# Row maxima and low-part scores of a two-mixer attention step, contracted over 64 rows and two heads at a time

## The chip, the cores and the metric

The kernel runs on one core of one Trainium2 chip. The metric is the device time of one execution in microseconds (us); before the change the median of three runs is 723.58 us. A core has five engines that run side by side, each in the order of its own instruction queue: PE (TensorE, the matrix multiplier: a matmul is a weight load followed by a stream of moving columns), DVE (VectorE), ACT (ScalarE), POOL (GpSimd) and SP, which here only issues DMAs. PE writes its results to PSUM, which has eight banks of 128 partitions by 512 float32; DVE and ACT read them there.

## The reference

One layer of a diffusion step: 128 context tokens and 1024 latent tokens are normalised, modulated, projected into queries, keys, values and gates of two mixers, attended, gated and projected out. Mixer A has 8 query heads on 2 key heads and looks at all keys; mixer B has as many, looks at a band of 128 to each side and adds a learned sink to each head's softmax. Both look at 128 cached context keys too. A head has 64 dimensions. Cut to what matters here:

```
def one_block(qblk):                       # mixer A, 128 queries, k_all = context and 1024 latent keys
    s = jnp.einsum('bqkgd,bskd->bkgqs', qblk, k_all).astype(jnp.float32) * (d ** -0.5)
    p = jax.nn.softmax(s, axis=-1).astype(v_all.dtype)
    return jnp.einsum('bkgqs,bskd->bqkgd', p, v_all)

# mixer B, banded blocks of 128 queries and up to 3 * 128 keys, and the context
s = jnp.concatenate([sink_column(sink, kv, s_ctx.shape[:-1]), s_ctx, s_band], axis=-1)
p = jax.nn.softmax(s, axis=-1).astype(v_lat.dtype)
o = p_ctx @ v_ctx + p_band @ v_band        # as einsums in the reference
```

Everything is float32.

## The kernel before

**Numbers.** PE multiplies a rounded float32 type. A float32 value is therefore kept as a high part, rounded to that type, and a low part, the rest. A query tile `qt` has 128 partitions and 4 heads of 128 queries: rows 0 to 63 hold the high part of the 64 dimensions, rows 64 to 127 the low part. The high keys `kha` (mixer A) and `khb` (mixer B) and the low keys of mixer B `klb` are stored twice, in rows 0 to 63 and again in rows 64 to 127. So one matmul over all 128 rows gives (high + low query) times high key; a second one over the low key completes a score.

**Units, slots.** The attention is cut into units: a block of 128 queries, a mixer, a key head (4 query heads). Units of mixer A (even numbers) and of mixer B (odd) alternate; 32 of latent queries, and 4 of the context. A unit of mixer A has nine slots, one for each block of 128 keys; one of mixer B has three or four. The main loop goes slot by slot and writes, for each, in this order on every engine: callbacks that fell due (`tick`), the slot's scores (`scores`), the items that a table put there (`due`), two or three matmuls of the output projection (`out_items`, line 1189), and the values (`values`, lines 1118 to 1121) of the slot three places back. The order is written out by hand in this way and each engine keeps it; nothing is rescheduled later.

**Scores of mixer A** are computed with keys on the partitions (lines 1097, 1098), exponentiated by ACT (1100), cut in two parts by ACT (1104) and POOL (1108), and multiplied with the values. A softmax needs a shift that is at or near the maximum of a row. It is made one unit ahead by `max_items`: for each of 4 heads and each of 3 groups of 384 keys a matmul with queries on the partitions (`pmx`, line 858) and a DVE reduction (859); twelve such items a unit. Their negated maxima are turned round by PE (`ptm`, 877) and spread by DVE into four rows of the tile `qb` (878), which is the moving operand of line 1098.

**Scores of mixer B** are made in `weight_items` with queries on the partitions, one head an item: a matmul with `khb` (915) and one with `klb` (916) into the same bank, a DVE operation that adds the mask and finds the negated row maximum (919), and one slot later ACT's exponential (905). The weights are turned round by PE (1092) in the unit's own slots, and the sums by `pti` (967).

**Banks.** Tag "A" of PSUM has two banks, handed out in turn. The maxima, the scores of mixer B, `ptm` and `pti` all use them: PE can start on the next one only when DVE or ACT has read the one before the last.

**Places.** `MX_AT` gives the slot of each maximum item, counted from the start of the mixer A unit before it; `NAT_AT` the slots of mixer B's items, counted from the start of the mixer A unit ahead. The items of units 0 and 2 run between the matmuls of the gate projection, before the slots. Query tiles are loaded by one DMA of SP each (838), at least five slots ahead of their first use.

Of the kernel before, what the change touches and what calls it, by code (L numbers as in the profile page):

```python
# [18 lines left out]
P = 128  # L19
# [20 lines left out]
LOADED = 4  # L40


NAT_AT = (0, 1, 2, 3)
NAT_FIRST = (0, 1, 2, 3)
MX_AT = (-4, -3, -2, -2, -1, 4, 5, 5, 7, 7, 8, 8)
MX_FIRST = (0, 1, 2, 2, 3, 4, 4, 5, 6, 6, 7, 8)
PH_DVE = 0
MX_END = 10
SPLIT_LAG = 2
# [58 lines left out]
def hybrid_step(ctx, tc, x_prompt, x_sample, cache_k_a, cache_v_a, cache_k_b, cache_v_b,  # L108
# [33 lines left out]
    def bank(tag, name):  # L142
        return ps.tile([P, 512], F32, tag=tag, name=name, bufs=BANKS[tag])
# [690 lines left out]
    def u_load(i):  # L834
        t, m, g = units[i]
        more = i % QTS > 3
        qt_ = (qp2[0] if more else qp).tile([P, 512], F32R, tag="qt", name=f"qt{i}", bufs=QTS - 4 if more else 4)
        nc.sync.dma_start(qt_.bitcast(F32), q_dram[t][m][:, 512 * g : 512 * g + 512])
        qtile[i] = qt_

    def max_items(i):

        t, m, g = units[i]
        out = []

        def item(h, b):
            if h == 0 and b == 0:
                mxtile[i] = qs.tile([P, 4, 3], F32, tag="mx", name=f"mx{i}", bufs=3)
            mx = mxtile[i]
            lhs = qtile[i][:, P * h : P * h + P]  # L850
            pm = bank("A", f"pmx{i}_{h}_{b}")
            if t == 0:
                for h in range(4):
                    hs = slice(P * h, P * h + P)
                    nc.tensor.matmul(pm[:, hs], qtile[i][:, hs], khp[:, g, :], start=True, stop=True)
                nc.vector.tensor_reduce(mx[:, :, 0], pm.rearrange("p (h n) -> p h n", h=4), axis=AX.X, op=ALU.max)
            else:
                nc.tensor.matmul(pm[:, 0:384], lhs, kha[:, g, 3 * b : 3 * b + 3, :], start=True, stop=True)  # L858
                nc.vector.tensor_reduce(mx[:, h, b : b + 1], pm[:, 0:384], axis=AX.X, op=ALU.max)  # L859

        def finish():
            qb_ = qp.tile([68, 512], F32R, tag="qb", name=f"qb{i}", bufs=2)
            nc.sync.dma_start(qb_[0:64, :].bitcast(F32), q_dram[t][m][0:64, 512 * g : 512 * g + 512])
            qbtile[i] = qb_
            mx = mxtile.pop(i)
            mn = m_nat[i // 2 % 2]
            if t > 0:
                m4 = qs.tile([P, 4], F32, tag="m4", name=f"m4{i}", bufs=3)
                nc.vector.tensor_reduce(m4, mx, axis=AX.X, op=ALU.max)
            else:  # L870
                m4 = mx[:, :, 0]
            nc.vector.tensor_scalar(mn, m4, -1.0, None, op0=ALU.mult)
            later(TURN, transpose)

        def transpose():
            pt = bank("A", f"ptm{i}")
            nc.tensor.transpose(pt[0:4, 0:P].bitcast(F32R), m_nat[i // 2 % 2], ident_r)
            nc.vector.tensor_tensor(qbtile[i][64:68, :].rearrange("p (h n) -> p h n", h=4),  # L878
                                    pt[0:4, 0:P].unsqueeze(1).to_broadcast([4, 4, P]),
                                    diag.unsqueeze(2).to_broadcast([4, 4, P]), op=ALU.mult)  # L880

        for h in range(4 if t else 1):
            for b in range(3 if t > 0 else 1):
                out.append(lambda h=h, b=b: item(h, b))
        return out, finish

    def weight_items(i):

        t, m, g = units[i]
        v = {}  # L890

        def small(name):
            return qs.tile([P, 4], F32, tag=name, name=f"{name}{i}")

        def first(n):
            if t:
                penat[i] = qp2[0].tile([P, 4, 512], F32, tag="pen", name=f"pen{i}")[:, :, 0:n]
            else:
                penat[i] = w3.tile([P, 512], F32, tag="pe", name=f"pen{i}", bufs=PES).rearrange(
                    "p (h n) -> p h n", h=4)  # L900
            for x in ("nm", "sum", "ex", "inv"):
                v[x] = small(x)

        def exp(h, s, scale):
            nc.scalar.activation(penat[i][:, h], s, AF.Exp, bias=v["nm"][:, h : h + 1], scale=scale,  # L905
                                 accum_out=v["sum"][:, h : h + 1])

        def item(h):
            p0, p1_ = window(t)
            n = P * (p1_ - p0)  # L910
            if h == 0:
                first(n)
            lhs = qtile[i][:, P * h : P * h + P]
            s = bank("A", f"sn{i}_{h}")[:, 0:n]
            nc.tensor.matmul(s, lhs, khb[:, g, p0:p1_, :], start=True, stop=False)
            nc.tensor.matmul(s, lhs, klb[:, g, p0:p1_, :], start=False, stop=True)  # L916
            m0 = P if t == 1 else 0

            nc.vector.tensor_tensor_reduce(s, s, mask[:, m0 : m0 + n], -1.0, nsink[:, 4 * g + h : 4 * g + h + 1],  # L919
                                           op0=ALU.add, op1=ALU.min, accum_out=v["nm"][:, h : h + 1])  # L920
            later(1, lambda: exp(h, s, -1.0))

        def prompt():
            first(P)
            s = bank("A", f"sn{i}")
            for h in range(4):
                hs = slice(P * h, P * h + P)
                nc.tensor.matmul(s[:, hs], qtile[i][:, hs], khp[:, 2 + g, :], start=True, stop=False)
                nc.tensor.matmul(s[:, hs], qtile[i][:, hs], klp[:, 2 + g, :], start=False, stop=True)
            mx = small("mx4")  # L930
            nc.vector.tensor_reduce(mx, s.rearrange("p (h n) -> p h n", h=4), axis=AX.X, op=ALU.max)
            nc.vector.scalar_tensor_tensor(v["nm"], mx, -1.0, nsink[:, 4 * g : 4 * g + 4], op0=ALU.mult, op1=ALU.min)
            for h in range(4):
                exp(h, s[:, P * h : P * h + P], 1.0)

        def finish():
            nc.gpsimd.tensor_tensor(v["ex"], v["nm"], sink[:, 4 * g : 4 * g + 4], op=ALU.add)
            if t:
                later(EX_AT[0], sinks)
                later(EX_AT[1], total)  # L940
                later(EX_AT[2], divide)
            else:
                sinks()
                later(1, total)
                later(1, divide)

        def sinks():
            nc.scalar.activation(v["ex"], v["ex"], AF.Exp)

        def total():  # L950
            nc.gpsimd.tensor_tensor(v["sum"], v["sum"], v["ex"], op=ALU.add)

        def divide():
            nc.vector.reciprocal(v["inv"], v["sum"])
            if t == 0:
                for h in range(4):
                    nc.vector.tensor_scalar(penat[i][:, h], penat[i][:, h], v["inv"][:, h : h + 1], None, op0=ALU.mult)
                return

            later(ROWS_AT[0], turned)  # L960
            later(ROWS_AT[1], put)
            later(ROWS_AT[2], rows)
            later(ROWS_AT[3], lambda: nc.gpsimd.tensor_tensor(sgl[i], sgl[i], v["rows"], op=ALU.mult))

        def turned():
            v["pt"] = bank("A", f"pti{i}")[0:4, 0:P]
            nc.tensor.transpose(v["pt"], v["inv"], ident_r.bitcast(F32))

        def put():
            iv = spare[0:4, 512 : 512 + P]  # L970
            nc.scalar.copy(iv, v["pt"])
            nc.sync.dma_start(r_dram[i // 2], iv)

        def rows():
            v["rows"] = spare[:, 512:768].rearrange("p (c n) -> p c n", c=2)
            for s in range(2):
                nc.sync.dma_start(v["rows"][HD * s : HD * s + HD],
                                  r_dram[i // 2].rearrange("(c s) n -> s c n", s=2)[s : s + 1].to_broadcast([HD, 2, P]))

        return ([lambda h=h: item(h) for h in range(4)] if t else [prompt]), finish  # L980


    wo_raw, wo_parts, wo_big = {}, {}, {}
# [231 lines left out]
    for i, (t, m, g) in enumerate(units):  # L1215
        if i in EARLY:
            continue
        if m == 0:
            items, done = max_items(i)
            at, end = [start[i - 2] + a for a in (MX_AT if i > 2 else MX_FIRST)], start[i - 2] + MX_END  # L1220
            if t == 0:
                end = start[i] - LEAD
                at = [end - 1]
        else:
            items, done = weight_items(i)
            at = [start[i - 1] + j for j in (NAT_AT if i > 1 else NAT_FIRST)] if t else [start[i] - PROMPT_LEAD]
            end = at[-1] + 1
        if i >= LOADED:
            first = max(start[i - QTS + 1] - 1, at[0] - LOADLEAD, 0)
            assert first < at[0] or first == 0, (i, first, at)  # L1230
# [92 lines left out]
```

## Time and profile before

| what | value |
|---|---|
| runs | 723.54, 723.58, 723.71 us |
| profiled execution, first to last instruction | 721.3 us, granted TensorE clock 0.993 |
| PE busy | 698.3 us (97%), 3524 matmuls |
| PE weight loads | 559.7 us (78%) |
| DVE, ACT, POOL busy | 457.6, 411.7, 335.3 us |
| DMA | 78.56 MB, mean 109 GB/s |

The profiled execution is one run; of it the page gives the span, and its time as the device counts it is not listed apart. The span is 2.3 us below the median of the runs. In the profile a row of a group reads: line of the kernel, engine, operation, what it writes and reads (buffer numbers left out), shape, count, then busy time in us, mean ns of one, and the idle time of the engine ahead of it with what ended it. "128\*64" on a PE row is active rows by active columns of the array. The ends of matmuls are modelled and one starts before the other has ended, so the pace of PE is read from the distance between two starts, not from a row's duration.

### The profile page before, as it was taken

How to read it: one execution, taken by the hardware profiler on the slowest of the kernel's cores; microseconds unless marked ns; L12 is line 12 of the kernel's file. 1: busy time of each engine (PE TensorE's matmuls, PEld its weight loads, DVE VectorE, ACT ScalarE, POOL GpSimd, SP SyncE). 2: the span in 40 equal slices, each digit the busy share in tenths (PEclk: the TensorE clock that was granted, in tenths of full speed). 3: DMA queues.
4: the chain of work that ended last, by engine and by line, in shares of the span. 5: the costliest groups of instructions: out<-in, count | busy, mean ns of one | idle time of the engine just before them, and what ended most of it. 6: DMA issues, size and time to landing. Idle time of an engine off the chain costs nothing. (4 is left out here: it accounts for less than half of the span.)

```text
span 721.3 us, 10622 instructions
## 1 busy us (share of the span) xinstructions
PE 698.3 (97%) x3524; PEld 559.7 (78%) x3524; DVE 457.6 (63%) x1007; ACT 411.7 (57%) x829; POOL 335.3 (46%) x355
## 2 busy tenths in 40 slices
PE   5999999999999999999999999999999999999997
PEld 2678988877777788977788888888888888887865
DVE  3466147875675872745866677577666775775653
ACT  5355411411232451158778877877787778877770
POOL 3456013332322340236666555655575557555751
PEclk9999999999999999999999999999999999999999
DMA  8961373348435115440321222121212221212323
GB/s 344 346 219 59 121 278 86 79 94 276 121 85 142 45 60 171 139 143 23 103 67 45 73 67 88 44 81 52 87 54 59 66 87 45 81 53 87 103 65 119
DMA packets 53159, 78.56 MB, mean 109 GB/s; under 512 B 6569, under 2 KB 25449, under 8 KB 52081
## 3 DMA queue, kind: packets, MB, share of 16 engines
q1 hardware_dynamic: 44928, 65.96, 28.1%
q10 hardware_dynamic: 8176, 11.94, 6.3%
q8 instruction: 28, 0.46, 0.3%
q14 instruction: 27, 0.21, 0.1%
HBM read 58.69 MB, written 19.18 MB: 108 GB/s over the span
## 5 line engine op out<-in xcount | busy, mean ns | idle before, releaser
L1108 POOL TENSOR_TENSOR pl<-pe,ph 128x512 fp32r<-128x512 f32 x130 | 167.6, 1292 | 144.7 <-DVE nm L919 67.5
L859 DVE TENSOR_REDUCE mx<-pmx 128x1 f32<-128x384 f32 x192 | 101.4, 552 | 59.5 <-PE pmx L858 58.1
L1100 ACT ACTIVATE pe<-st 128x512 f32<-128x512 f32 x146 | 86.8, 594 | 28.0 <-PE st L1098 27.1
L1104 ACT CAST ph<-pe 128x512 fp32r<-128x512 f32 x146 | 90.6, 621 | 4.8
L1118 PE MATMUL pv<-ph,v_hi 128*128 128x512 f32 x208 | 83.2, 400 | 2.2 <-DVE spare L1142 2.2
L1121 PE MATMUL pv<-pl,v_hi 128*128 128x512 f32 x208 | 82.6, 397 | 0.0
L173 POOL TENSOR_TENSOR rs_q<-ms_q,mhalf 128x8 f32<-128x8 f32 x18 | 34.8, 1931 | 82.1 <-DVE ms_q L171 82.1
L1189 PE MATMUL po<-wo,ogh 128*128 128x512 f32 x216 | 72.5, 394 | 0.2 <-DVE yt L1196 0.2
L919 DVE CUSTOM_DVE_ANT_0 sn<-sn,mask,nsink 128x512 f32<-128x512 f32 (+1 forms) x64 | 46.3, 724 | 38.3 <-PE sn L916 36.5
L858 PE MATMUL pmx<-kha,qt 128*128 128x384 f32 x192 | 61.0, 363 | 0.4 <-ACT pen L905 0.2
L1097 PE MATMUL st<-qt,kha 128*128 128x512 f32 x144 | 58.3, 405 | 1.5 <-ACT pe L1100 0.8
L1098 PE MATMUL st<-qb,kla 68*128 68x512 f32 x144 | 57.6, 400 | 1.1 <-DVE qb L878 1.1
L1120 PE MATMUL pv<-ph,v_lo 128*64 128x512 f32 x146 | 57.9, 396 | 0.0
L1121 PEld LDWEIGHTS pv<-pl,v_hi 128*128 128x128 f32 x208 | 39.4, 189 | 16.7 <-issue 0.2
L905 ACT ACTIVATE pen<-sn,nm 128x512 f32<-128x512 f32 (+2 forms) x72 | 45.0, 626 | 6.5 <-DVE nm L919 3.1
L1093 ACT CAST ph<-st 128x512 fp32r<-128x512 f32 x62 | 36.4, 587 | 19.9 <-PE st L1092 18.7
L1118 PEld LDWEIGHTS pv<-ph,v_hi 128*128 128x128 f32 x208 | 39.4, 189 | 10.5 <-ACT ogh L1154 2.4
L1189 PEld LDWEIGHTS po<-wo,ogh 128*128 128x128 f32 x216 | 40.0, 188 | 6.8 <-DVE yt L1196 0.6
L1094 DVE TENSOR_TENSOR pl<-st,ph 128x512 fp32r<-128x512 f32 x62 | 42.5, 686 | 2.3 <-ACT ph L1093 1.5
L1189 PE MATMUL po<-wo,ogl 128*128 128x512 f32 x108 | 42.6, 394 | 0.0
L594 ACT ACTIVATE sqq<-pq 128x512 f32<-128x512 f32 x18 | 10.8, 599 | 53.3 <-DMA qd<-qo0q 14.4
L858 PEld LDWEIGHTS pmx<-kha,qt 128*128 128x128 f32 x192 | 35.5, 190 | 6.2 <-DVE mx L859 1.4
(216 smaller groups left out, 1700.2 us busy)
## 6 DMA issues: line engine op xcount, KB each, us to landing
qt<-qd SPq DMA_DIRECT2D x36, 256.0 KB, 3.1
wm<-in_w_mod_ss_dram SPq DMA_DIRECT2D x8, 1024.0 KB, 5.1
qd<-qo0q ACTq DMA_DIRECT2D x36, 128.0 KB, 2.4
qd<-qo1q ACTq DMA_DIRECT2D x36, 128.0 KB, 2.4
sgl<-gd SPq DMA_DIRECT2D x36, 128.0 KB, 2.1
out_dram<-yt SPq DMA_DIRECT2D x17, 256.0 KB, 2.1
xn<-in_x_sample_dram SPq DMA_DIRECT2D x8, 512.0 KB, 7.0
wg<-in_w_mod_g_dram SPq DMA_DIRECT2D x4, 1024.0 KB, 7.9
```

What stands on the lines that cost most here:

```text
L858: nc.tensor.matmul(pm[:, 0:384], lhs, kha[:, g, 3 * b : 3 * b + 3, :], start=True, stop=True)
L859: nc.vector.tensor_reduce(mx[:, h, b : b + 1], pm[:, 0:384], axis=AX.X, op=ALU.max)
L919: nc.vector.tensor_tensor_reduce(s, s, mask[:, m0 : m0 + n], -1.0, nsink[:, 4 * g + h : 4 * g + h + 1], op0=ALU.add, op1=ALU.min, accum_ou ...
L1097: nc.tensor.matmul(s, kh, qtile[i], start=True, stop=False)
L1098: nc.tensor.matmul(s, kl, qbtile[i], start=False, stop=True)
L1100: nc.scalar.activation(pe, s, AF.Exp)
L1104: nc.scalar.copy(ph, pe)
L1108: nc.gpsimd.tensor_tensor(pl, pe, ph, op=ALU.subtract)
L1118: nc.tensor.matmul(pv, two, ph, start=(b == 0), stop=False)
L1120: nc.tensor.matmul(pv[0:64, :], vl, ph, start=False, stop=False)
L1121: nc.tensor.matmul(pv, two, pl, start=False, stop=last)
L1189: nc.tensor.matmul(po[n], a, wo_parts[KT * n + k][lo], start=(k == KS[0] and p == 0), stop=(k == KS[-1] and p == 2))
```

## The change

The maxima of mixer A now contract 64 rows, the high part of the queries with the high part of the keys, and two heads are done by two matmuls that stand one behind the other, one on rows 0 to 63 of the array and one on rows 64 to 127. For that the odd heads of a query tile are loaded with their halves exchanged (low part in rows 0 to 63, high part in rows 64 to 127), by two further DMAs. `kha` and `khb` hold the same in both halves, so the matmuls over all 128 rows are the same sum as before. The low-part scores of mixer B contract 64 rows in the same way: high query times low key, where before the low query times the low key was in the sum too. So an item of `max_items` is now two heads (six items a unit), and an item of `weight_items` two heads (two a unit); the two exponentials of an item follow one another in ACT's queue. `MX_AT` and `NAT_AT` have a place for each item of two heads; `finish` of mixer B's unit stays at the fourth slot.

```diff
--- before.py
+++ after.py
@@ -40,10 +40,9 @@
 LOADED = 4
 
 
-NAT_AT = (0, 1, 2, 3)
-NAT_FIRST = (0, 1, 2, 3)
-MX_AT = (-4, -3, -2, -2, -1, 4, 5, 5, 7, 7, 8, 8)
-MX_FIRST = (0, 1, 2, 2, 3, 4, 4, 5, 6, 6, 7, 8)
+NAT_AT = (0, 2)
+NAT_END = 4
+MX_AT = (-4, -3, -1, 4, 6, 8)
 PH_DVE = 0
 MX_END = 10
 SPLIT_LAG = 2
@@ -835,28 +834,38 @@
         t, m, g = units[i]
         more = i % QTS > 3
         qt_ = (qp2[0] if more else qp).tile([P, 512], F32R, tag="qt", name=f"qt{i}", bufs=QTS - 4 if more else 4)
-        nc.sync.dma_start(qt_.bitcast(F32), q_dram[t][m][:, 512 * g : 512 * g + 512])
+        to = qt_.bitcast(F32).rearrange("r (p s n) -> r p s n", s=2, n=P)
+        src = q_dram[t][m][:, 512 * g : 512 * g + 512].rearrange("r (p s n) -> r p s n", s=2, n=P)
+        nc.sync.dma_start(to[:, :, 0], src[:, :, 0])
+        for a in (0, 64):
+            nc.sync.dma_start(to[a : a + 64, :, 1], src[64 - a : 128 - a, :, 1])
         qtile[i] = qt_
 
+    def by_rows(i, p, keys):
+
+        return [(qtile[i][64 * s : 64 * s + 64, P * (2 * p + s) : P * (2 * p + s) + P], keys[64 * s : 64 * s + 64])
+                for s in range(2)]
+
     def max_items(i):
 
         t, m, g = units[i]
-        out = []
-
-        def item(h, b):
-            if h == 0 and b == 0:
+
+        def prompt():
+            mxtile[i] = mx = qs.tile([P, 4, 3], F32, tag="mx", name=f"mx{i}", bufs=3)
+            pm = bank("A", f"pmx{i}")
+            for h in range(4):
+                hs = slice(P * h, P * h + P)
+                nc.tensor.matmul(pm[:, hs], qtile[i][:, hs], khp[:, g, :], start=True, stop=True)
+            nc.vector.tensor_reduce(mx[:, :, 0], pm.rearrange("p (h n) -> p h n", h=4), axis=AX.X, op=ALU.max)
+
+        def item(p, b):
+            if p == 0 and b == 0:
                 mxtile[i] = qs.tile([P, 4, 3], F32, tag="mx", name=f"mx{i}", bufs=3)
-            mx = mxtile[i]
-            lhs = qtile[i][:, P * h : P * h + P]
-            pm = bank("A", f"pmx{i}_{h}_{b}")
-            if t == 0:
-                for h in range(4):
-                    hs = slice(P * h, P * h + P)
-                    nc.tensor.matmul(pm[:, hs], qtile[i][:, hs], khp[:, g, :], start=True, stop=True)
-                nc.vector.tensor_reduce(mx[:, :, 0], pm.rearrange("p (h n) -> p h n", h=4), axis=AX.X, op=ALU.max)
-            else:
-                nc.tensor.matmul(pm[:, 0:384], lhs, kha[:, g, 3 * b : 3 * b + 3, :], start=True, stop=True)
-                nc.vector.tensor_reduce(mx[:, h, b : b + 1], pm[:, 0:384], axis=AX.X, op=ALU.max)
+            pms = [bank("A", f"pmx{i}_{2 * p + s}_{b}")[:, 0:384] for s in range(2)]
+            for pm, (q, k) in zip(pms, by_rows(i, p, kha[:, g, 3 * b : 3 * b + 3, :])):
+                nc.tensor.matmul(pm, q, k, start=True, stop=True)
+            for s in range(2):
+                nc.vector.tensor_reduce(mxtile[i][:, 2 * p + s, b : b + 1], pms[s], axis=AX.X, op=ALU.max)
 
         def finish():
             qb_ = qp.tile([68, 512], F32R, tag="qb", name=f"qb{i}", bufs=2)
@@ -879,10 +888,7 @@
                                     pt[0:4, 0:P].unsqueeze(1).to_broadcast([4, 4, P]),
                                     diag.unsqueeze(2).to_broadcast([4, 4, P]), op=ALU.mult)
 
-        for h in range(4 if t else 1):
-            for b in range(3 if t > 0 else 1):
-                out.append(lambda h=h, b=b: item(h, b))
-        return out, finish
+        return ([lambda p=p, b=b: item(p, b) for p in range(2) for b in range(3)] if t else [prompt]), finish
 
     def weight_items(i):
 
@@ -905,20 +911,22 @@
             nc.scalar.activation(penat[i][:, h], s, AF.Exp, bias=v["nm"][:, h : h + 1], scale=scale,
                                  accum_out=v["sum"][:, h : h + 1])
 
-        def item(h):
+        def item(p):
             p0, p1_ = window(t)
             n = P * (p1_ - p0)
-            if h == 0:
+            if p == 0:
                 first(n)
-            lhs = qtile[i][:, P * h : P * h + P]
-            s = bank("A", f"sn{i}_{h}")[:, 0:n]
-            nc.tensor.matmul(s, lhs, khb[:, g, p0:p1_, :], start=True, stop=False)
-            nc.tensor.matmul(s, lhs, klb[:, g, p0:p1_, :], start=False, stop=True)
+            heads = (2 * p, 2 * p + 1)
+            ss = [bank("A", f"sn{i}_{h}")[:, 0:n] for h in heads]
+            for h, s in zip(heads, ss):
+                nc.tensor.matmul(s, qtile[i][:, P * h : P * h + P], khb[:, g, p0:p1_, :], start=True, stop=False)
+            for s, (q, k) in zip(ss, by_rows(i, p, klb[:, g, p0:p1_, :])):
+                nc.tensor.matmul(s, q, k, start=False, stop=True)
             m0 = P if t == 1 else 0
-
-            nc.vector.tensor_tensor_reduce(s, s, mask[:, m0 : m0 + n], -1.0, nsink[:, 4 * g + h : 4 * g + h + 1],
-                                           op0=ALU.add, op1=ALU.min, accum_out=v["nm"][:, h : h + 1])
-            later(1, lambda: exp(h, s, -1.0))
+            for h, s in zip(heads, ss):
+                nc.vector.tensor_tensor_reduce(s, s, mask[:, m0 : m0 + n], -1.0, nsink[:, 4 * g + h : 4 * g + h + 1],
+                                               op0=ALU.add, op1=ALU.min, accum_out=v["nm"][:, h : h + 1])
+            later(1, lambda: [exp(h, s, -1.0) for h, s in zip(heads, ss)])
 
         def prompt():
             first(P)
@@ -977,7 +985,7 @@
                 nc.sync.dma_start(v["rows"][HD * s : HD * s + HD],
                                   r_dram[i // 2].rearrange("(c s) n -> s c n", s=2)[s : s + 1].to_broadcast([HD, 2, P]))
 
-        return ([lambda h=h: item(h) for h in range(4)] if t else [prompt]), finish
+        return ([lambda p=p: item(p) for p in range(2)] if t else [prompt]), finish
 
 
     wo_raw, wo_parts, wo_big = {}, {}, {}
@@ -1217,14 +1225,14 @@
             continue
         if m == 0:
             items, done = max_items(i)
-            at, end = [start[i - 2] + a for a in (MX_AT if i > 2 else MX_FIRST)], start[i - 2] + MX_END
+            at, end = [start[i - 2] + a for a in MX_AT], start[i - 2] + MX_END
             if t == 0:
                 end = start[i] - LEAD
                 at = [end - 1]
         else:
             items, done = weight_items(i)
-            at = [start[i - 1] + j for j in (NAT_AT if i > 1 else NAT_FIRST)] if t else [start[i] - PROMPT_LEAD]
-            end = at[-1] + 1
+            at = [start[i - 1] + j for j in NAT_AT] if t else [start[i] - PROMPT_LEAD]
+            end = start[i - 1] + NAT_END if t else at[-1] + 1
         if i >= LOADED:
             first = max(start[i - QTS + 1] - 1, at[0] - LOADLEAD, 0)
             assert first < at[0] or first == 0, (i, first, at)
```

Three places in the order that the kernel writes, with what stands there before and after. In the names, `pmx12_1_0` is the maxima of unit 12, head 1, key group 0.

PE, the slots of mixer B's unit 9, in which the maxima of unit 12 begin; before:

```order
L1092 MATMUL st9_1_4676<-ident_r_99,pen9_4464 128x128 x4
L858 MATMUL pmx12_0_1_4689<-kha_2319,qt12_4560 128x384
...
L1092 MATMUL st9_2_4696<-ident_r_99,pen9_4464 128x128 x4
L858 MATMUL pmx12_0_2_4704<-kha_2319,qt12_4560 128x384
L858 MATMUL pmx12_1_0_4707<-kha_2319,qt12_4560 128x384
...
L877 MATMUL ptm10_4719<-ident_r_99,m_nat1_109 4x128
L1092 MATMUL st9_3_4726<-ident_r_99,pen9_4464 128x128 x4
L858 MATMUL pmx12_1_1_4734<-kha_2319,qt12_4560 128x384
```

and now:

```order
L1100 MATMUL st9_1_4705<-ident_r_99,pen9_4489 128x128 x4
L866 MATMUL pmx12_0_1_4718<-kha_2319,qt12_4588 128x384
L866 MATMUL pmx12_1_1_4719<-kha_2319,qt12_4588 128x384
...
L1100 MATMUL st9_2_4728<-ident_r_99,pen9_4489 128x128 x4
...
L886 MATMUL ptm10_4745<-ident_r_99,m_nat1_109 4x128
L1100 MATMUL st9_3_4752<-ident_r_99,pen9_4489 128x128 x4
L866 MATMUL pmx12_0_2_4760<-kha_2319,qt12_4588 128x384
L866 MATMUL pmx12_1_2_4761<-kha_2319,qt12_4588 128x384
```

The second slot now has two matmuls of one pair where it had one; the third has none where it had two; in the last, behind `ptm`, there is a pair where there was a single one.

DVE at the same place, before:

```order
L869 TENSOR_REDUCE m410_4686<-mx10_4376 128x4
L872 TENSOR_SCALAR m_nat1_109<-m410_4686 128x4
L859 TENSOR_REDUCE mx12_4664<-pmx12_0_1_4689 128x1
L1094 TENSOR_TENSOR pl9_1_4678<-st9_1_4676,ph9_1_4677 128x512
L859 TENSOR_REDUCE mx12_4664<-pmx12_0_2_4704 128x1
L859 TENSOR_REDUCE mx12_4664<-pmx12_1_0_4707 128x1
L878 TENSOR_TENSOR qb10_4684<-ptm10_4719,diag_110 4x512
```

and now:

```order
L878 TENSOR_REDUCE m410_4715<-mx10_4398 128x4
L881 TENSOR_SCALAR m_nat1_109<-m410_4715 128x4
L868 TENSOR_REDUCE mx12_4690<-pmx12_0_1_4718 128x1
L868 TENSOR_REDUCE mx12_4690<-pmx12_1_1_4719 128x1
L1102 TENSOR_TENSOR pl9_1_4707<-st9_1_4705,ph9_1_4706 128x512
L887 TENSOR_TENSOR qb10_4713<-ptm10_4745,diag_110 4x512
```

Two reductions stand ahead of `pl9_1` where there was one, and none between it and `qb10`.

PE, a step of mixer B's unit 11, in the first slots of unit 10; before, one head in each of two slots:

```order
L1098 MATMUL st10_0_4746<-qb10_4684,kla_2320 128x512
L915 MATMUL sn11_0_4760<-khb_2321,qt11_4649 128x512
L916 MATMUL sn11_0_4760<-klb_2322,qt11_4649 128x512
...
L915 MATMUL sn11_1_4778<-khb_2321,qt11_4649 128x512
L916 MATMUL sn11_1_4778<-klb_2322,qt11_4649 128x512
```

and now, both heads in one slot, with the two matmuls over 64 rows at the end:

```order
L1106 MATMUL st10_0_4775<-qb10_4713,kla_2320 128x512
L922 MATMUL sn11_0_4789<-khb_2321,qt11_4673 128x512
L922 MATMUL sn11_1_4790<-khb_2321,qt11_4673 128x512
L924 MATMUL sn11_0_4789<-klb_2322,qt11_4673 128x512
L924 MATMUL sn11_1_4790<-klb_2322,qt11_4673 128x512
```

Both banks of tag "A" are now taken in one slot, and DVE masks both heads there, one behind the other.

## The prediction

> **What bounds the kernel now.** I read the page's first part and its groups, then the table by stage, then the waits of PE, then the timeline of single slots. First the page:
>
> ```profile
> PE 698.3 (97%) x3524; PEld 559.7 (78%) x3524; DVE 457.6 (63%) x1007; ACT 411.7 (57%) x829; POOL 335.3 (46%) x355
> ...
> L858 PE MATMUL pmx<-kha,qt 128*128 128x384 f32 x192 | 61.0, 363 | 0.4 <-ACT pen L905 0.2 <-DVE mx L859 0.2
> ...
> L1120 PE MATMUL pv<-ph,v_lo 128*64 128x512 f32 x146 | 57.9, 396 | 0.0
> ```
>
> PE is busy 97% of the span. A share is an average, so the stages, two pieces from the middle of the attention:
>
> ```profile
> 389.00:411.00 22.00, 22.00 (x109) 17.68 (x108) 15.90 (x34) 16.89 (x34) 12.92 (x15) 1.00 0.19 58
> 433.00:455.00 22.00, 22.00 (x109) 17.67 (x108) 16.51 (x35) 17.11 (x35) 12.21 (x14) 1.00 0.24 72
> ```
>
> The columns behind the window are its length, then PE, weight loads, DVE, ACT, POOL, the clock and DMA. PE is busy 22.00 of 22 us at full clock; ACT, the next engine, 17.1. PE waits for others almost never (waits of PE from 320 us on, in us, times, longest):
>
> ```profile
> PE pv L1118 <- DVE spare L1142: 2.2, 4, 1.0
> PE st L1098 <- DVE qb L878: 1.1, 2, 0.6
> ```
>
> So in the attention a microsecond that PE saves is one of the kernel, until another wait takes it. What a matmul costs is the distance between starts:
>
> ```profile
> 327.50 0.40 PE L1098 MATMUL st<-qb,kla 68*128 68x512 f32 x1
> 327.73 0.34 PE L858 MATMUL pmx<-kha,qt 128*128 128x384 f32 x1
> 327.91 0.40 PE L1118 MATMUL pv<-ph,v_hi 128*128 128x512 f32 x1
> 328.14 0.40 PE L1120 MATMUL pv<-ph,v_lo 128*64 128x512 f32 x1
> 328.38 0.40 PE L1121 MATMUL pv<-pl,v_hi 128*128 128x512 f32 x1
> 328.61 0.60 PE L1092 MATMUL st<-ident_r,pen 128*128 128x128 f32 x4
> 328.97 0.42 PE L858 MATMUL pmx<-kha,qt 128*128 128x384 f32 x1
> 329.23 0.39 PE L1118 MATMUL pv<-ph,v_hi 128*128 128x512 f32 x1
> ```
>
> 512 columns take 0.23 us, 384 columns 0.175 (327.73 to 327.91), and four transposes with a maximum behind them 0.62, so 0.44 for the four.
>
> **What PE saves.** The 192 maxima become 96 pairs. If the two halves of a pair run side by side, a pair takes 0.175 where two took 0.35: 96 x 0.175 = 16.8 us. The low-part scores of mixer B:
>
> ```profile
> L916 PE MATMUL sn<-klb,qt 128*128 128x512 f32 x48 | 18.9, 394 | 0.0
> ...
> L916 PE MATMUL sn<-klb,qt 128*128 128x384 f32 x16 | 5.6, 348 | 0.0
> ```
>
> 24 pairs of 0.23 and 8 of 0.175: 6.9 us. Together 23.7. No row shows a pair on row halves, so two prices are open.
>
> First: do the halves overlap? Nearest row, strips of columns instead of rows:
>
> ```profile
> L350 PE MATMUL pm<-wm,sil 128*32 128x256 f32 x128 | 10.0, 437 | 0.0
> ```
>
> 128 records of 437 ns are 56 us, and took 10.0: the four strips run at once. Bounds: a second half costs from nothing to a full matmul (0.175 or 0.23). I take nothing, since these strips are the only row with tiles side by side, and keep the full matmul for the range.
>
> Second: what does it cost to go from the whole array to halves and back, 128 times? Lower bound, the rows above: L1120 uses 64 columns between matmuls with 128, and starts 0.23 after its predecessor and 0.24 before its successor; 146 such changes cost nothing. Upper bound, the true float32 matmuls on column strips:
>
> ```profile
> 18.04 0.40 PE L262 MATMUL pg_f<-h,whiga 128*128 128x512 f32 x1
> 18.28 0.39 PE L263 MATMUL pg_f<-h,wloga 128*128 128x512 f32 x1
> 18.59 1.66 PE L350 MATMUL pm<-wm,sil 128*32 128x256 f32 x16
> ...
> 194.61 1.02 PE L565 MATMUL pgs<-grow,selg 128*2 128x512 f32 x2
> 195.56 0.19 PEld L248 LDWEIGHTS pq<-whiqb,h 128*128 128x128 f32 x1 [0.86 <-issue]
> 195.56 0.50 PE L248 MATMUL pq<-whiqb,h 128*128 128x512 f32 x1
> 195.67 0.19 PEld L249 LDWEIGHTS pq<-wloqb,h 128*128 128x128 f32 x1
> 195.90 0.39 PE L249 MATMUL pq<-wloqb,h 128*128 128x512 f32 x1
> ```
>
> Going in, L350 starts 0.31 after its predecessor instead of 0.23. Coming out, L565's two records of 0.43 each end at 195.47, the next weights load only at 195.56 (0.09 lost), and not under the work before, so L249 starts 0.34 after L248 instead of 0.23 (0.11 more). That is about 0.2 us a change. Those rows differ from a pair in two things, column strips and the full float32 type; L1120 differs in one, and has the type of the pairs. So I take zero, and keep 0.2 for the range. The Trainium skill, "TensorEngine Tiling (Array Packing)", section "Key Properties", says that changing the tiling mode drains TensorE. The 146 changes of L1120 disagree, if a strip of 64 columns counts as a mode; by that sentence the result would be the slower rival below.
>
> **What the pairs add in waits.** A pair wants both banks of tag "A" at once, where a single matmul wanted one. Around the start of the next unit's maxima the trace shows how close DVE is:
>
> ```profile
> 419.08 0.51 PE L858 MATMUL pmx<-kha,qt 128*128 128x384 f32 x2
> 419.42 0.39 PE L1118 MATMUL pv<-ph,v_hi 128*128 128x512 f32 x1
> 419.45 1.02 DVE L859 TENSOR_REDUCE mx<-pmx 128x1 f32<-128x384 f32 x2 [0.96 <-PE pmx L858]
> ...
> 420.12 0.60 PE L1092 MATMUL st<-ident_r,pen 128*128 128x128 f32 x4
> ...
> 424.80 0.22 PE L877 MATMUL ptm<-ident_r,m_nat 128*4 128x128 f32 x1
> 424.86 0.60 PE L1092 MATMUL st<-ident_r,pen 128*128 128x128 f32 x4
> ...
> 425.06 0.68 DVE L878 TENSOR_TENSOR qb<-ptm,diag 4x512 fp32r<-4x512 f32 x1 [0.36 <-PE ptm L877]
> 425.21 0.42 PE L858 MATMUL pmx<-kha,qt 128*128 128x384 f32 x1
> ```
>
> Let a pair start at 0, in the last slot of a unit of mixer A. DVE starts 0.37 later and both banks are free at 0.37 + 1.02 = 1.39. PE is back after 0.175, the values (419.42 to 420.12, 0.70) and four transposes (0.44): at 1.32. The second half of the next pair waits some 0.1. In the next slot `pti` and a pair again need banks that DVE leaves at 2.4 and 2.9 and ACT after `pti`; I put 0.25 for both. Two slots on, `ptm` holds one bank until `qb` is written: 425.06 + 0.68 = 425.74. Before, the single maximum took the other bank at 425.21. A pair needs both: PE is ready 0.50 after `ptm` (0.06 and four transposes), the bank free 0.94 after it, so it waits 0.45 to 0.5. Behind the waiting half on PE stand the output projection and the values, and POOL, ACT and DVE behind those: nothing else fills the time. Together 0.85 to 0.9 in each of the 14 mixer A units whose maxima run in the slots (units 4 to 30): 12 us. It is an estimate of mine from these rows; its bounds are 0 (the waits fall where others already were) and 18 (if DVE is later by one more subtraction, 0.69, at half of the places):
>
> ```profile
> L1094 DVE TENSOR_TENSOR pl<-st,ph 128x512 fp32r<-128x512 f32 x62 | 42.5, 686 | 2.3 <-ACT ph L1093 1.5
> ...
> L919 DVE CUSTOM_DVE_ANT_0 sn<-sn,mask,nsink 128x512 f32<-128x512 f32 x48 | 36.4, 757 | 27.0 <-PE sn L916 26.8 <-ACT pen L905 0.2
> ```
>
> Mixer B's step of two heads puts both masks and both exponentials together. DVE has 16 of 22 us, ACT 17 of 22, and the results are needed two slots later; no price. If that cover is gone, it is one mask (the second of these rows, 0.76) per step, 24 us over 32 steps; I give it no weight.
>
> **DMAs.** 36 loads become 108 issues:
>
> ```profile
> qt<-qd SPq DMA_DIRECT2D x36, 256.0 KB, 3.1
> ...
> 417.48 0.42 SPq L838 DMA_DIRECT2D qt<-qd  x1
> ...
> 400.93 0.22 PE L877 MATMUL ptm<-ident_r,m_nat 128*4 128x128 f32 x1
> ```
>
> Two more issues of 0.42 us on SP delay the landing by 0.9 to 4.0 us. Loads stand at least five slots ahead: `ptm` recurs every 23.87 us (400.93, 424.80), which is 13 slots of a pair of units, so five are 9 us. Behind them in SP's queue wait the gate tiles and the sums' rows, a slot or more ahead of their use. No price; uncovered it would be 0.9 a load, 32 us.
>
> **Sum.** 23.7 saved, 12 given back: 11.7 us off. Against the profiled span, 721.3 becomes 709.6; the span lies 2.3 under the median of the runs (723.58), so 711.9. I say 712.
>
> **The rivals.**
> *The switches cost* (slower). Place: each of the 128 pairs; price 0.2 in, 0.2 out. 128 x 0.4 = 51 against 23.7 saved: +27.5; of the bank waits most then fall inside, +2: 753. It decides from 0.045 us a switch on, where 128 x 2 x 0.045 = 11.5 eats my gain. For it: L350 and L565; against: L1120.
> *The halves run one after another.* PE saves nothing; the second half comes 0.175 later, so about half of the waits stay: 723.6 + 6 = 730. For it: no row has row halves. Against: L350. The Trainium skill, "TensorE: Matmul & The Clock Gate", section "Part 3: Packing small matmuls — row/col tiling", has row tiles run concurrently; no run here shows it.
> *The waits do not come.* 723.6 - 23.7 = 700, up to 704. For it: DVE is idle 6 of 22 us. Against: the banks are handed out in turn, `qb` cannot come earlier than `ptm`.
>
> **How the numbers follow.** Forecast (overlap, free switches, bank waits) 0.48, own range 704 to 719. Switches 0.22, one after another 0.18, no waits 0.12. A measurement of this kernel tells 0.2%, 1.4 us, from no change. Faster: 0.48 + 0.12, less 0.03 for switches of just 0.045: 0.57. Same 0.05, those 0.03 and 0.02 from the second rival. Slower 0.38. The range 700 to 739 holds the forecast, most of the third, nearly all of the second rival, and of the first those with switches up to 0.1 us: about 0.8.
>
> **What would show it.** In the timeline: the two L866 of a pair starting within 0.02 us (0.175 apart: second rival). The start of L1126 after a pair: 0.18 after the pair if switches are free, 0.4 or more if not. In PE's waits: L866 on DVE `qb` and `mx`, together near 12 us; if below 2, the third rival; above 20, I have DVE too fast. ACT's waits at L911 should grow while PE does not wait for it. If loads of `qt` appear among PE's waits, the DMA step was wrong.

## The result, and the profile after

The changed kernel takes 755.16 us, median of four runs (754.21 to 756.73); the kernel before took 723.56 beside it. The ratio is 1.0436, 95% interval 1.0413 to 1.0460: 31.6 us slower. The forecast was 712 with a range of 700 to 739. The profiled run took 755.51 us with a span of 753.7.

The page of the changed kernel, first part and groups (the lines of the code have moved by 8 or 9: the maxima's matmul is 866, its reduction 868, mixer B's matmuls 922 and 924):

```profile
PE 727.0 (96%) x3524; PEld 536.2 (71%) x3524; DVE 454.4 (60%) x1007; ACT 410.9 (55%) x829; POOL 336.0 (45%) x355
...
L1126 PEld LDWEIGHTS pv<-ph,v_hi 128*128 128x128 f32 x208 | 39.3, 189 | 20.7 <-issue 10.7
...
L866 PE MATMUL pmx<-kha,qt 64*128 64x384 f32 x192 | 48.0, 437 | 2.1 <-DVE mx L868 2.0
...
L866 PEld LDWEIGHTS pmx<-kha,qt 64*128 64x128 f32 x192 | 20.4, 183 | 30.3 <-issue 10.1
```

PE counts as many matmuls as before and 29 us more of busy time. DVE, ACT and POOL have what they had, within 3.2 us. What is new stands on the weight loads: idle time ahead of them that ended with "issue", that is, with nothing the profile shows: 10.7 us at the first matmul of the values, 10.1 at the maxima themselves. The same two groups before had 10.5 and 6.2 us of idle time in all, with other engines named first:

```profile
L1118 PEld LDWEIGHTS pv<-ph,v_hi 128*128 128x128 f32 x208 | 39.4, 189 | 10.5 <-ACT ogh L1154 2.4
...
L858 PEld LDWEIGHTS pmx<-kha,qt 128*128 128x128 f32 x192 | 35.5, 190 | 6.2 <-DVE mx L859 1.4
```

The table by stage in the middle of the attention (columns: length, PE, weight loads, DVE, ACT, POOL, clock, DMA share, GB/s):

```profile
400.00:422.00 22.00, 22.00 (x101) 15.11 (x100) 14.99 (x33) 14.90 (x31) 11.37 (x13) 1.00 0.16 46
440.00:462.00 22.00, 22.00 (x99) 15.10 (x98) 15.02 (x33) 16.45 (x34) 14.03 (x15) 1.00 0.23 66
```

PE is still busy 22.00 of 22, but with 100 matmuls where there were 109, at full clock. A PE that loses time in this way still looks full; the weight loads, down from 17.7 to 15.1, tell it. Waits of PE from 300 us on (us, times, longest) are much what they were in this view; it leaves out one that matters, which the first experiment brings up:

```profile
PE pv L1126 <- DVE spare L1150: 2.9, 4, 1.1
PE st L1106 <- DMA qb<-qd: 0.8, 1, 0.8
PE ptm L886 <- DVE mx L868: 0.6, 1, 0.6
PE pmx L866 <- DVE mx L868: 0.6, 1, 0.6
```

And one pair in the timeline:

```profile
400.32 0.40 PE L1105 MATMUL st<-qt,kha 128*128 128x512 f32 x1
400.55 0.40 PE L1106 MATMUL st<-qb,kla 68*128 68x512 f32 x1
400.88 0.44 PE L866 MATMUL pmx<-kha,qt 64*128 64x384 f32 x2
401.25 0.19 PEld L1197 LDWEIGHTS po<-wo_big,ogl 128*128 128x128 f32 x1 [0.18 <-issue]
401.25 0.50 PE L1197 MATMUL po<-wo_big,ogl 128*128 128x512 f32 x1
401.36 0.19 PEld L1197 LDWEIGHTS po<-wo_big,ogh 128*128 128x128 f32 x1
401.59 0.39 PE L1197 MATMUL po<-wo_big,ogh 128*128 128x512 f32 x1
```

The two matmuls of the pair are one row of 0.44 us: a single one of them has 0.437 by its group above, so they start together. The halves do run side by side. But the pair starts 0.33 after its predecessor, not 0.23; the next weights load 0.37 after the pair, where a pair's stream is 0.16 to 0.19 (measured below, with pairs in a row); and the matmul behind starts 0.34 later instead of 0.23, since its weights' load did not hide under the pair. From L1106 to the second L1197 it is 1.04 us. By the paces of before (0.23, two maxima of 0.175, 0.23) it was 0.81. So a pair costs 0.23 more than the two matmuls that it replaced, although its own halves overlap.

### The profile page after: what moved, and what is told of

It reads as the page before. It is cut to its first block, busy times and chain, and to the rows that moved or that the text cites. A ratio compares the mean times of both kernels' runs of the same rounds, so it can differ in the third digit from the quotient of the medians.

```text
span 753.7 us, 10744 instructions
## 1 busy us (share of the span) xinstructions
PE 727.0 (96%) x3524; PEld 536.2 (71%) x3524; DVE 454.4 (60%) x1007; ACT 410.9 (55%) x829; POOL 336.0 (45%) x355
## 5 line engine op out<-in xcount | busy, mean ns | idle before, releaser
L868 DVE TENSOR_REDUCE mx<-pmx 128x1 f32<-128x384 f32 x192 | 97.9, 551 | 70.3 <-PE pmx L866 69.1
L1126 PE MATMUL pv<-ph,v_hi 128*128 128x512 f32 x208 | 88.1, 424 | 3.0 <-DVE spare L1150 2.9
L1197 PE MATMUL po<-wo,ogh 128*128 128x512 f32 x216 | 76.7, 414 | 0.2 <-DVE yt L1204 0.2
L927 DVE CUSTOM_DVE_ANT_0 sn<-sn,mask,nsink 128x512 f32<-128x512 f32 (+1 forms) x64 | 44.7, 723 | 47.4 <-PE sn L924 47.4
L1106 PE MATMUL st<-qb,kla 68*128 68x512 f32 x144 | 57.7, 401 | 1.3 <-DMA qb<-qd 0.8
L1126 PEld LDWEIGHTS pv<-ph,v_hi 128*128 128x128 f32 x208 | 39.3, 189 | 20.7 <-issue 10.7
L1101 ACT CAST ph<-st 128x512 fp32r<-128x512 f32 x62 | 36.3, 586 | 28.4 <-PE st L1100 28.1
L866 PE MATMUL pmx<-kha,qt 64*128 64x384 f32 x192 | 48.0, 437 | 2.1 <-DVE mx L868 2.0
L1197 PEld LDWEIGHTS po<-wo,ogh 128*128 128x128 f32 x216 | 38.5, 189 | 11.4 <-issue 5.9
L1197 PE MATMUL po<-wo,ogl 128*128 128x512 f32 x108 | 45.4, 420 | 0.0
L866 PEld LDWEIGHTS pmx<-kha,qt 64*128 64x128 f32 x192 | 20.4, 183 | 30.3 <-issue 10.1
```

The source lines that it names most:

```text
L866: nc.tensor.matmul(pm, q, k, start=True, stop=True)
L868: nc.vector.tensor_reduce(mxtile[i][:, 2 * p + s, b : b + 1], pms[s], axis=AX.X, op=ALU.max)
L1106: nc.tensor.matmul(s, kl, qbtile[i], start=False, stop=True)
L1126: nc.tensor.matmul(pv, two, ph, start=(b == 0), stop=False)
L1197: nc.tensor.matmul(po[n], a, wo_parts[KT * n + k][lo], start=(k == KS[0] and p == 0), stop=(k == KS[-1] and p == 2))
```

## The experiments

Two theories stood after the result. **Switch**: every change between the whole array and row halves stops the stream (0.10 us, and 0.11 for weights that load in the open), twice a pair. **Order**: the step of two heads, with two banks at once and three loads a tile, costs the time. The second is what my prediction had priced, at 12 us.

### Whole rows in the new order

```diff
-        return [(qtile[i][64 * s : 64 * s + 64, P * (2 * p + s) : P * (2 * p + s) + P], keys[64 * s : 64 * s + 64])
-                for s in range(2)]
+        return [(qtile[i][:, P * (2 * p + s) : P * (2 * p + s) + P], keys) for s in range(2)]
```

> The changed kernel with its order, its three loads a query tile and its two banks a step, but every matmul of a pair over all 128 rows, as before. If the changes between whole array and row halves are the cost (0.10 us going in, 0.30 coming out, of which 0.11 is the next weights' load that no longer hides), about 26 of the 32 us go away and what stays is order and banks: 727 to 731. If the two banks a step or the loads are the cost, it stays at 755 or gets worse, since nothing runs side by side any more: 755 to 779.

Measured: 730.99 us beside 723.08 of the kernel before (ratio 1.0099, 1.0072 to 1.0126). So the order and the loads cost 7.9 us, and the row halves the other 24. Where the order loses it is seen in this kernel's timeline, PE and DVE, in the last slot of a unit of mixer B:

```profile
427.62 0.22 PE L885 MATMUL ptm<-ident_r,m_nat 128*4 128x128 f32 x1
427.68 0.60 PE L1099 MATMUL st<-ident_r,pen 128*128 128x128 f32 x4
...
427.89 0.68 DVE L886 TENSOR_TENSOR qb<-ptm,diag 4x512 fp32r<-4x512 f32 x1 [0.71 <-PE ptm L885]
428.04 0.42 PE L865 MATMUL pmx<-kha,qt 128*128 128x384 f32 x1
...
428.62 0.44 PE L865 MATMUL pmx<-kha,qt 128*128 128x384 f32 x1 [0.16 <-DVE qb L886]
```

and among its waits of PE:

```profile
PE pmx L865 <- DVE qb L886: 1.9, 12, 0.2
```

The second maximum starts 0.58 after the first, not 0.175, because `qb` still holds the bank: 0.40 lost, as the prediction had it for this place (0.45 to 0.5). The wait comes 12 times, 4.8 us in all (the view counts 0.16 of each as idle, since the modelled end of the first maximum covers the rest). The three other places that I had priced at 0.35 show no loss here.

The changed kernel has the same wait, 12 times as well. At the same place its two halves do not start together, but 0.40 apart, so that the merged row of the pair has 0.84 us and not 0.44:

```profile
411.27 0.68 DVE L887 TENSOR_TENSOR qb<-ptm,diag 4x512 fp32r<-4x512 f32 x1 [0.96 <-PE ptm L886]
...
411.61 0.84 PE L866 MATMUL pmx<-kha,qt 64*128 64x384 f32 x2
...
412.01 0.18 PEld L866 LDWEIGHTS pmx<-kha,qt 64*128 64x128 f32 x1 [0.23 <-DVE qb L887]
...
412.38 0.50 PE L1197 MATMUL po<-wo,ogl 128*128 128x512 f32 x1
```

PE's waits do not list it, because the modelled end of the first half (0.44) covers all of the 0.40. The waits of the weight loads do (from 300 us on):

```profile
PEld pmx L866 <- DVE qb L887: 2.7, 12, 0.2
```

So 4.8 us of the 7.9 are this wait, in both kernels, and 1.9 are the loads (measured below). The 1.2 us left are no more than single runs of one kernel differ by.

### Only the maxima, only mixer B

In the new order, one of the two on row halves and the other over whole rows:

Only the maxima:

```diff
-            for s, (q, k) in zip(ss, by_rows(i, p, klb[:, g, p0:p1_, :])):
-                nc.tensor.matmul(s, q, k, start=False, stop=True)
+            for h, s in zip(heads, ss):
+                nc.tensor.matmul(s, qtile[i][:, P * h : P * h + P], klb[:, g, p0:p1_, :], start=False, stop=True)
```

Only mixer B:

```diff
-            for pm, (q, k) in zip(pms, by_rows(i, p, kha[:, g, 3 * b : 3 * b + 3, :])):
-                nc.tensor.matmul(pm, q, k, start=True, stop=True)
+            for s, pm in enumerate(pms):
+                lhs = qtile[i][:, P * (2 * p + s) : P * (2 * p + s) + P]
+                nc.tensor.matmul(pm, lhs, kha[:, g, 3 * b : 3 * b + 3, :], start=True, stop=True)
```

> Only the maxima of mixer A on row halves (96 pairs); the low parts of mixer B over whole rows, in the changed order. Switches: 96 x (0.40 - 0.175) = 21.6 on top of the kernel with whole rows, about 750. If mixer B's step of two heads were the cost: below 735.

> Only mixer B's low parts on row halves (32 pairs); the maxima over whole rows, in the changed order. Switches: 24 x (0.40 - 0.23) + 8 x (0.40 - 0.175) = 5.9 on top of the kernel with whole rows, about 735. If mixer B's part were the cost: about 750.

Measured, on the same chip: 749.38 (ratio 1.0353, 1.0326 to 1.0381) and 735.96 (1.0167, 1.0139 to 1.0194). Over whole rows that is 18.4 for 96 pairs and 5.0 for 32: 0.19 and 0.16 a pair. The two add up to 23.4, and the changed kernel lies 24.2 above whole rows. The loss goes with the number of pairs, not with the mixer. It is a little less than the 21.6 and 5.9 that were expected; the spans of the profiled executions (728.3, 748.5 and 734.4) differ by 20.2 and 6.1.

### Only the loads

```diff
-        nc.sync.dma_start(qt_.bitcast(F32), q_dram[t][m][:, 512 * g : 512 * g + 512])
+        nc.sync.dma_start(to[:, :, 0], src[:, :, 0])
+        for a in (0, 64):
+            nc.sync.dma_start(to[a : a + 64, :, 1], src[64 - a : 128 - a, :, 1])
```

> The kernel before, with nothing changed but the loads of query tiles (three DMAs, odd heads with exchanged halves; the sums are the same). Switches: 723.6, within 1. If the loads are late or in the way: up to 32 us more.

Measured: 724.93, ratio 1.0024 (1.0008 to 1.0039), 1.9 us more; small, but not the nothing that I had put. Its profile has one wait of PE that the kernel before does not have, ahead of the slots, while the gate projection runs. First SP's queue before, then with the three loads, then DVE and PE of the latter:

```profile
278.25 0.33 SPq L1020 DMA_DIRECT2D mask<-in_k_mask_dram  x1
278.75 1.76 SPq L838 DMA_DIRECT2D qt<-qd  x4
282.52 1.76 SPq L998 DMA_DIRECT2D wraw<-in_w_out_dram  x4
```

```profile
279.55 0.33 SPq L1024 DMA_DIRECT2D mask<-in_k_mask_dram  x1
280.05 0.37 SPq L840 DMA_DIRECT2D qt<-qd  x1
...
286.26 1.22 SPq L842 DMA_DIRECT2D qt<-qd  x2
287.59 1.95 SPq L1002 DMA_DIRECT2D wraw<-in_w_out_dram  x4
```

```profile
290.66 0.43 DVE L1018 CAST wo<-wraw 128x512 fp32r<-128x512 f32 x1 [2.01 <-DMA wraw<-in_w_out_dram]
...
291.73 1.02 DVE L863 TENSOR_REDUCE mx<-pmx 128x1 f32<-128x384 f32 x2
...
292.34 0.44 PE L862 MATMUL pmx<-kha,qt 128*128 128x384 f32 x1 [1.44 <-DVE mx L863]
```

The first four tiles are twelve DMAs in a row, and the output weights behind them in SP's queue leave 8.0 us after the mask, where they left 4.3 us after it: 3.8 us later. DVE waits 2.0 us for them, in order, with reductions queued behind, and PE 1.4 us for those. The changed kernel has the same wait (1.4 us, PE on `mx` before 300 us). In the slots this kernel's PE waits for no DMA; the changed kernel's does once, 0.8 us for the rows of `qb`, as the list of its waits above shows.

### Both matmuls in one half

The pair on rows 0 to 63 both times, loaded by one DMA:

```diff
-        to = qt_.bitcast(F32).rearrange("r (p s n) -> r p s n", s=2, n=P)
-        src = q_dram[t][m][:, 512 * g : 512 * g + 512].rearrange("r (p s n) -> r p s n", s=2, n=P)
-        nc.sync.dma_start(to[:, :, 0], src[:, :, 0])
-        for a in (0, 64):
-            nc.sync.dma_start(to[a : a + 64, :, 1], src[64 - a : 128 - a, :, 1])
+        nc.sync.dma_start(qt_.bitcast(F32), q_dram[t][m][:, 512 * g : 512 * g + 512])
...
-        return [(qtile[i][64 * s : 64 * s + 64, P * (2 * p + s) : P * (2 * p + s) + P], keys[64 * s : 64 * s + 64])
-                for s in range(2)]
+        return [(qtile[i][0:64, P * (2 * p + s) : P * (2 * p + s) + P], keys[0:64]) for s in range(2)]
```

> The changed kernel, but both matmuls of a pair on rows 0 to 63 (high query, high or low key; the tiles loaded by one DMA, unexchanged), so the two run one after another in the same row half. If the price is the change between whole array and a half, it stays at 0.40 and the second matmul's time comes on top: 96 x 0.16 + 24 x 0.21 + 8 x 0.16 = 22, 755 + 22 = 775 to 779. If it needs two halves at work or a place other than row 0, the price goes: about 731, the kernel with whole rows in this order.

Measured: 776.61 (774.15 and 779.06; ratio 1.0750, 1.0602 to 1.0898, beside 722.43), 21.4 over the changed kernel, where 22 is the stream of 128 second matmuls. The two runs lie 5 us apart, and this kernel is spared the extra loads (1.9 us above), so the 21.4 is good to a few us. The timeline shows the price itself:

```profile
399.03 0.40 PE L1101 MATMUL st<-qb,kla 68*128 68x512 f32 x1
399.36 0.61 PE L861 MATMUL pmx<-kha,qt 64*128 64x384 f32 x2
399.91 0.74 PE L1192 MATMUL po<-wo,ogh 128*128 128x512 f32 x2
```

The first of the two again starts 0.33 after its predecessor, and the work behind follows 0.55 after it, 0.18 more than the 0.37 of a pair side by side. So the price does not hang on two halves at work, nor on the place in the array: 64 rows at row 0 are enough. And side by side is worth about what the sum had for it. The matmul ahead, L1101, has 68 active rows, and such a matmul pays nothing: in the changed kernel L1106 starts 0.23 after its predecessor (400.32 to 400.55), and before the change L1098 started 0.23 before its successor (327.50 to 327.73 in the prediction's rows). So fewer rows than 128 are not the price as such.

### Pairs in a row

Each pair of maxima issued twice, or three times, into the same banks, and the same three times over whole rows:

```diff
-            for pm, (q, k) in zip(pms, by_rows(i, p, kha[:, g, 3 * b : 3 * b + 3, :])):
-                nc.tensor.matmul(pm, q, k, start=True, stop=True)
+            for _ in range(3):
+                for pm, (q, k) in zip(pms, by_rows(i, p, kha[:, g, 3 * b : 3 * b + 3, :])):
+                    nc.tensor.matmul(pm, q, k, start=True, stop=True)
```

(`range(2)` for twice; over whole rows `by_rows` is changed as in the first experiment.)

> The changed kernel with each pair of maxima issued twice in a row into the same two banks (the second overwrites the same values). If the price is one change in and one out, the second pair costs only its stream, 0.16 to 0.18: 96 x 0.17 = 16, about 771. If every pair drains the array: 96 x 0.40 = 38, about 793.

> Whole rows in the changed order, each step's two maxima issued three times in a row (the last one counts): what six whole-row matmuls in a row cost. 96 x 4 x 0.175 = 67 over the kernel with whole rows once (731), less the 5 to 6 us of bank waits that may fall inside: 792 to 798.

> The changed kernel with each pair of maxima issued three times in a row: the same maxima as in the kernel with six whole-row matmuls, on row halves. If the price is one change in and out, each further pair costs 0.16: 755 + 96 x 2 x 0.16 = 786, below the kernel with whole rows thrice, since from 0.40 / (0.35 - 0.16) = 2.1 pairs in a row on the halves win (mixer B's 32 single pairs still lose 5). If pairs are dear in themselves: above 800.

Measured: pairs twice 770.42 (ratio 1.0664, 1.0618 to 1.0710); pairs thrice 789.11 (1.0900, 1.0864 to 1.0937); whole rows thrice 796.47 (1.1002, 1.0962 to 1.1042). From the changed kernel, a second pair in a row costs (770.42 - 755.16) / 96 = 0.16 us, a third one (789.11 - 770.42) / 96 = 0.19; over whole rows each further two maxima cost (796.47 - 730.99) / 192 = 0.34. These subtract runs that were not taken side by side; the kernel before took 722.43 to 723.56 beside them, so they are good to about 0.02. A further pair thus costs about what a single maximum took before (0.175), and not the 0.40 on top: the price is per change of mode. With three pairs in a row the halves win by 7.4 us, as the break-even of 2.1 said; the time of 789 is 3 over the 786 expected. Two pairs in a row were not run over whole rows. First the kernel with each pair twice, then pairs thrice and whole rows thrice, at the same kind of place:

```profile
407.03 0.40 PE L1107 MATMUL st<-qb,kla 68*128 68x512 f32 x1
407.36 0.62 PE L867 MATMUL pmx<-kha,qt 64*128 64x384 f32 x4
407.91 0.50 PE L1127 MATMUL pv<-ph,v_hi 128*128 128x512 f32 x1
```

```profile
414.20 0.40 PE L1107 MATMUL st<-qb,kla 68*128 68x512 f32 x1
414.53 0.80 PE L867 MATMUL pmx<-kha,qt 64*128 64x384 f32 x6
415.26 0.49 PE L1127 MATMUL pv<-ph,v_hi 128*128 128x512 f32 x1
```

```profile
417.54 0.40 PE L1106 MATMUL st<-qb,kla 68*128 68x512 f32 x1
417.77 1.22 PE L866 MATMUL pmx<-kha,qt 128*128 128x384 f32 x6
418.83 0.39 PE L1126 MATMUL pv<-ph,v_hi 128*128 128x512 f32 x1
```

Going in takes 0.33 each time on the halves; from the first pair to the next matmul it is 0.37 for one pair, 0.55 for two, 0.73 for three: 0.18 for each further pair. Six whole-row maxima take 1.06.

A kernel that gains from this would need three or more pairs in a row, hence six banks at once for the maxima. Two of the eight are theirs; the others hold the scores, the values and the output projection throughout the slots. I found no version that beats the kernel before, and ran none.

### Does the type matter?

The prediction had set the values' low part (64 columns, rounded type, no price) against L565 and L350 (strips of 2 and of 32 columns, true float32, 0.2 us a change), and two things differ between them. So the low part as true float32, same place and columns:

```diff
-            nc.tensor.matmul(pv[0:64, :], vl, ph, start=False, stop=False)
+            nc.tensor.matmul(pv[0:64, :], vl.bitcast(F32), ph.bitcast(F32), start=False, stop=False)
```

> The kernel before with the 146 matmuls of 64 columns (values' low part) read as true float32 instead of the rounded type; same columns, same place in the array. Its use is in the trace: if the type makes the change dear, the start after such a matmul and the load behind it come late by 0.09 and 0.11, as at L565; if only strips do it, the starts follow without a gap. The time rises in both cases by 146 x 0.63 = 92 for the longer stream, and by 146 x 0.3 = 44 more if the type is it: about 815 or 859.

Measured: 863.56 in one run, 5 over the 859 expected. Its timeline:

```profile
418.71 0.40 PE L1118 MATMUL pv<-ph,v_hi 128*128 128x512 f32 x1
419.04 0.19 PEld L1120 LDWEIGHTS pv<-ph,v_lo 128*64 128x64 f32 x2 [0.37 <-issue]
419.04 1.07 PE L1120 MATMUL pv<-ph,v_lo 128*64 128x512 f32 x2
420.04 0.19 PEld L1121 LDWEIGHTS pv<-pl,v_hi 128*128 128x128 f32 x1 [0.81 <-issue]
420.04 0.50 PE L1121 MATMUL pv<-pl,v_hi 128*128 128x512 f32 x1
420.15 0.19 PEld L1097 LDWEIGHTS st<-qt,kha 128*128 128x128 f32 x1
420.38 0.39 PE L1097 MATMUL st<-qt,kha 128*128 128x512 f32 x1
```

Now L1120 starts 0.33 after L1118, and L1097 0.34 after L1121, the signs of the changed kernel's pair. By the time it is (863.56 - 722.43) / 146 = 0.97 for each of these matmuls, 0.34 more than the 0.63 of the longer stream, where a visit to the row halves costs 0.40. So for these matmuls the type alone makes the change dear; the row halves make it dear in the rounded type. What the two have in common is not shown. Nor does the type do it everywhere: the transposes of line 1092 of the kernel before are read as true float32 too (`ident_r.bitcast(F32)`), and in the prediction's rows the first of four starts 0.23 after a full matmul (328.38, 328.61), with no sign of the price. Strips of columns at another place, in the rounded type, were not tried.

## Why the prediction was wrong, point by point

- **What bounds the kernel**: right, as far as the runs go. What is added on PE is added to the kernel: a second stream per pair moved the median by 21.4 us, a further pair by its stream. No run took time off PE.
- **What PE saves**: the overlap was right. The two records of a pair start together, and putting both into one half costs 21.4 us, near the 23.7 that the sum had. (L350 was not the only row of before with strips at once: L573 has 32 records of 598 ns in 3.8 us of busy time.)
- **The price of a switch**: this is the step that failed. "So I take zero, and keep 0.2 for the range": the runs show 0.2 each way, 0.40 a visit, 128 visits. I took zero from a row that shared the type but not the thing that changes: 64 columns at column 0 do not show what 64 rows do. A row can bound a price only if it has the property that is new; of two rows that both differ, I had no ground to take the cheaper one as the value. With 0.2 the sum was on the page: the rival had 753 and the measurement is 755.16. But that the dearer rows had the right number is in part luck. L350 and L565 have no row halves either; they differ by column strips and by true float32, and the last experiment shows that this type by itself can make the price. The rival's 753 also had most of the bank waits fall away (2 us left), where 4.8 us of them are there.
- **The range**: the rival's chance was 0.22 and its time outside; "of the first those with switches up to 0.1 us". The known upper bound of an unknown price belonged inside.
- **The Trainium skill's rule**, "TensorEngine Tiling (Array Packing)", section "Key Properties", that a change of tiling mode drains TensorE: the runs agree with it for row halves, where time is lost both ways (0.33 for 0.23 going in, 0.37 for some 0.17 until the next weights load). I had let L1120 speak against it.
- **Waits for banks**: 12 us were forecast. The one at `qb` is there, with whole rows and in the changed kernel alike, at 12 of the 14 units, 0.40 each, 4.8 us; those at the three other places are not. The mechanism was right at one place of four. The sign that I had named, PE's waits of L866 on `qb` and `mx` below 2 us for no waits at all, would have misled: from 300 us on that view has 0.6 us, because it counts only the idle time behind the modelled end of the matmul ahead.
- **The step of two heads in mixer B**: no price, and none seen: of the order's 7.9 us only 1.2 are left beside the wait at `qb` and the loads, and its 32 pairs cost 5.0 us over whole rows, which the switches explain (5.9 expected).
- **Loads**: forecast nothing; 1.9 us (0.6 to 2.8 by the interval). The three issues of a tile take 1.9 us of SP's queue where one took 0.44, and not the 0.84 more that the prediction had for two of 0.42. I had looked at what waits for the tiles in the slots, and not at the four first loads that stand in a row ahead of the output weights in SP's queue.
- **The sum as it is**: 18.4 for the maxima's pairs and 5.0 for mixer B's by the two separate runs; 7.9 for the order with its loads, of which 4.8 are the wait at `qb` and 1.9 the loads. Together 31.3 of 31.6.

## What to carry to other kernels

Two half-height matmuls side by side do take the time of one, but each visit to that mode costs about 0.4 us here, and three pairs in a row gained where single pairs lost, so count the visits before packing single pairs into a stream of full matmuls. A PE that is busy all the time by the profile can still be losing it: compare the matmuls in a window and the weight loads' busy time, and look for "issue" as what ended the idle time before a load. And a wait of PE can hide behind the modelled end of the matmul ahead of it: look at the waits of the weight loads, and at the distance between starts, before saying that it is gone.

## What the runs showed of the hardware

- A change between whole array and row halves costs 0.10 us each way (start 0.33 for 0.23 going in), and 0.11 more each way because the first weights behind it do not load under the matmuls ahead of it (the second L1197 0.34 after the first, for 0.23).
- Within the mode nothing is lost that shows: a further pair of 384 columns costs 0.16 to 0.19 us, where a single maximum over whole rows took 0.175.
- Both matmuls on the same 64 rows pay the same price (0.33 going in, in the kernel with both in one half), so it does not take two halves at work; 68 rows pay none (0.23 from start to start at L1098).
- Going from the rounded float32 type to true float32 and back costs nearly as much (0.34 us a visit, one run), with no change of rows, at 64 of 128 columns; the transposes of line 1092, read as true float32, show no such price (0.23 after a full matmul).
